# Gate rows through TensorE and PSUM instead of a scatter, and sums and dot products placed behind low parts on VectorE

## The chip, the cores and the metric

The kernel runs on one core of a Trainium2 chip. A core has five engines that run their own instruction lists side by side: PE (TensorE, matmuls; PEld is its weight load), DVE (VectorE), ACT (ScalarE), POOL (GpSimd) and SP (SyncE, which here does nothing but issue transfers). 16 DMA engines move data between the memory of the chip (HBM) and the core's own memories: SBUF (128 partitions) and PSUM (where matmuls accumulate). The metric is the device time of one execution in microseconds (us), lower is better.

## The reference, cut to what matters

One layer of a diffusion transformer: 512 tokens x and 256 context tokens ctx, width 1024, all in float32. A conditioning vector is turned into shifts, scales and gates (nine sections of 1024 numbers for x, from `c`; the same for ctx, from `c_ctx`); they multiply and shift the tokens before a sublayer and scale what the sublayer adds.

```
mod_x = (silu(c) @ w_ada + b_ada).reshape(bsz, N_MOD, 1, d)      # N_MOD = 9
mod_c = (silu(c_ctx) @ w_ada + b_ada).reshape(N_MOD, 1, d)

def ffn_sublayer(h, m, i, w_up, w_down):
    shift, scale, gate = sub_mod(m, i)
    y = swiglu(modulate(h, shift, scale), w_up, w_down)
    return post_ln(DEEPNORM_ALPHA * h + 0.5 * gate * y, ln_g[i], ln_b[i])

x   = ffn_sublayer(x,   mod_x, 0, ffn1_w_in, ffn1_w_out)         # d_ff 2816
ctx = ffn_sublayer(ctx, mod_c, 0, ffn1_w_in, ffn1_w_out)
...                                                              # projections, attention, gated DeltaNet, merge
x   = ffn_sublayer(x,   mod_x, 2, ffn2_w_in, ffn2_w_out)
```

The change touches only how the gates are brought into rows, and when the dot products for `w_ada` and some sums for the first sublayer run. Nothing of what is computed changes.

## The kernel before, in words

**Products in three parts.** Every float32 weight tile that is loaded (128x1024, 512 KB) is split in two: ACT casts a high part (`wh`, the line with `S.copy` in `split`, L137 in the profile) and DVE subtracts it to get a low part (`wl`, L139). Activations are split likewise (`uh`/`ul`, `hx`/`hl`). A product is then three matmuls: high by high, high by low, low by high (L192, L193, L194 in the up-projections, L211 in the down-projections, L521 to L523 in `Seven`). So PE cannot use a weight tile until DVE has made its low part.

**Stages** (by the trace of before): start and modulation of x to 57 us; up-projection of x for the first 8 blocks of the hidden width, the last five of them in 57 to 118 us (called x-up below); the same 8 for ctx, 256 columns wide, 118 to 166 us (ctx-up); the down-projection of x for these 8 to about 226 us (x-down) and of ctx to about 250 us; then 14 blocks for x by a seven-product scheme, class `Seven`, to 460 us; their down-projection for x to 540 us and for ctx until about 600 us with the first layer norms (post_ln, L255 on); projections and convolution to 840 us; gated DeltaNet and attention to 1140 us; merge, second FFN and its down-projection to the end.

**Modulation by dot products.** A section of the conditioning needs 8 tiles of `w_ada` (already transposed, `w_adaT`). The first two sections are done at the start. The other seven come from the generator `ada_gen`: one step (`ada_step`) loads one 512 KB tile by the SP queue (L295) and takes its dot product on DVE (`dot_cols`, L279, a 128x1024 multiply with a running sum) for x and, for sections 2 to 4, a second one for ctx. Steps are called where the other work is expected to leave DVE time: ADA2 and ADA3 list how many per block of `Seven` and per block of the down-projection after it. The result is a column tile: element n of a section lies at partition n % 128, column n // 128.

**Gate rows.** Gates are needed as rows (1024 numbers, the same on all partitions). `to_row` (L239 to L243) halves the 128x8 column tile on ACT into a tile `row`, writes it to HBM with one transfer on SP's queue (`gate<-row`, L243), transposed by its addresses: 128x8 elements of four bytes each. Four rows go this way: section 2 for x and for ctx, section 5 and section 8 for x. `load_g` (L560) and `bcast_row` (L246) later load a row back to all partitions.

**Sums of token blocks.** `Seven` needs sums and differences of blocks of the modulated x tokens: `sums(k)` (L461 and the splits behind it) makes them in four calls, each of four subtractions and four splits: 32 DVE instructions of 128x384 or so in all.

**What sets the order.** The kernel is written with pools of named buffers, and a scheduler that simulates the program by its own estimates of each operation sets the order of the instructions on each engine; buffers of one name are reused in turn, so a load can wait for a reader. `tc.issue_after(x)` puts an instruction behind instruction x in that order. All weight loads, `w_adaT` loads and gate rows share SP's one queue of issues.

Of the kernel before, what the change touches and what calls it, by code (L numbers as in the profile page):

```python
# [10 lines left out]
F32 = mybir.dt.float32  # L11
F32R = mybir.dt.float32r
AF = mybir.ActivationFunctionType
ALU = mybir.AluOpType
# [4 lines left out]
P = 128  # L19
D = 1024  # L20
KT = D // P
# [37 lines left out]
def body(ctx, tc, I, out, dbg=None):  # L59
    nc = tc.nc  # L60
    V, S, G, T = nc.vector, nc.scalar, nc.gpsimd, nc.tensor
# [15 lines left out]
    def tl(p, shape, tag, bufs=1, dt=F32):  # L77
        uid[0] += 1
        return p.tile(list(shape), dt, name=f"{tag}_{uid[0]}", tag=tag, bufs=bufs)
# [54 lines left out]
    def split(src, hi, lo, behind=()):  # L134

        with tc.issue_after(behind[0]) if behind and behind[0] else nullcontext():
            S.copy(hi, src)  # L137
        with tc.issue_after(behind[1]) if behind else nullcontext():
            V.tensor_tensor(lo, src, hi.bitcast(F32), ALU.subtract)  # L139

# [97 lines left out]

    def to_row(sp, cols, row):  # L239

        t = tl(sp, [P, KT], "row")
        S.activation(t[:], cols, AF.Copy, scale=0.5)
        nc.sync.dma_start(row.rearrange("k p -> p k"), t[:])  # L243

# [44 lines left out]
    def ada_gen(tps, raw_of, crow):  # L289
        for sec in range(2, 9):  # L290
            which = [(0, colx)] + ([(1, colc)] if sec < 5 else [])
            sl = slice(sec * 8, sec * 8 + 8)
            for k in range(KT):
                raw = raw_of[0]()
                nc.sync.dma_start(raw[:], I["w_adaT"][sec * KT + k])  # L295
                for w, col in which:
                    dot_cols(tps[0], raw, crow[:, w], col, sec * 8 + k)
                if k < KT - 1:
                    yield
            for w, col in which:  # L300
                V.scalar_tensor_tensor(col[:, sl], col[:, sl], float(sec % 3 == 1), bcol[:, sl], op0=ALU.add, op1=ALU.add)
                if (w, sec) in gates:
                    to_row(tps[0], col[:, sl], gates[(w, sec)])
            yield
# [77 lines left out]
    F0, KC, KL1, KL2 = 3, 2, 6, 6  # L382
    ADA2 = (2,) * 13 + (0,)
    ADA3 = (3, 3, 3, 2, 2, 2, 2, 2)
    PSB = [2]
# [55 lines left out]
    gates = {k: tl(dp, [8, P], "gate")[:] for k in ((0, 2), (1, 2), (0, 5), (0, 8))}  # L441
    ada_tp, ada_raw = [tp], [raw1]
    ada = ada_gen(ada_tp, ada_raw, crow)

    def ada_step(n=1):
        for _ in range(n):
            next(ada, None)

    for f in range(F0, N1):
        hx.append(h_x())  # L450
        ffn_unit(tp, pp, ws.get(), ws.get(), uxh, uxl, NX, *hx[-1])
        for k in range(KC * (f - F0), min(KC * (f - F0 + 1), KT)):
            modulate_k(pp, "c", k)
    ada_step()
    trow = {}
# [13 lines left out]
    for f in range(N1):  # L469
        hc.append(h_c())  # L470
        ffn_unit(tp, pp, ws.get(), ws.get(), uch, ucl, NCT, *hc[-1])
        ada_step(1 - f % 2)
    accd = tl(dp, [6, P, D], "accd")

    def t_sums(j):
        if j < 4:
            sums(j)
        ada_step()
        if j == 3:
            load_g(0)  # L480

    class Seven:
# [43 lines left out]
        def run(self, r):  # L526
# [20 lines left out]
            V.tensor_tensor(c21, c21, self.product(4), ALU.add)  # L547
            V.tensor_tensor(c1[:], c1[:], c2[:], ALU.mult)
            nc.gpsimd.dma_start(hd[self.f - N1].rearrange("p (a n) -> p a n", a=2), c1[:])
# [50 lines left out]
    for f in range(N2):  # L600
        fs[f].run(fs[f + 1] if f + 1 < N2 else None)
        if f + 2 < N2:
            fs.append(Seven(N1 + f + 2))
        ada_step(ADA2[f])
    close_sg()
# [81 lines left out]
    for t in range(4):  # L687
        evac1(lp, bx[t], accx[t], accx[t], gx)
    gc = tl(lp, [P, D], "g")
    bcast_row(gc, gates[(1, 2)])  # L690
# [1170 lines left out]
```

## Time and profile before

| what | before |
|---|---|
| three runs | 1543.77, 1543.99, 1548.96 us; median 1543.99 us |
| profiled execution | 1547.91 us, span of the instructions 1546.1 us, mean granted TensorE clock 0.980 |
| PE busy | 1447.1 us (94% of the span) |
| DVE busy | 1156.1 us (75%) |
| ACT / POOL busy | 648.7 us (42%) / 211.0 us (14%) |
| DMA | 248.03 MB, 160 GB/s over the span |

PE is busy nearly all of the time and can be slowed only by what it waits for and by its clock. The stages differ, though: in some, DVE is nearly as busy as PE. A row of a timeline reads: start, duration, engine, line, operation, out<-in, shapes, count, and in brackets how long the engine stood idle before and what released it. Matmul rows with a count cover several in a row. A row of the windows reads: stretch, its length, then for each engine the busy time and (in brackets) the instructions, the granted TensorE clock, the busy share of the DMA engines and their GB/s.

### The profile page before, as it was taken

Reading aid. Unit: us, or ns where it says so; the run is one execution under the profiler, and the core shown is the slowest. Engines: PE = TensorE matmul, PEld = TensorE weight load, DVE = VectorE, ACT = ScalarE, POOL = GpSimd, SP = SyncE. Lnnn points to the kernel's source line nnn. Section 1 sums busy time; section 2 is a strip of 40 time slices with the busy share of each in tenths; the row PEclk is TensorE's granted clock in tenths of the full one; section 3 lists DMA queues with packets and bytes.
Section 4 is the critical chain, followed back from the end, with each engine's and each line's share of the span. In section 5 each row is a group of like instructions: output and inputs, shape, how many; then the busy total and the mean of one; then the engine's idle time right before and its main releaser. Section 6 shows DMA issues by size and latency. Waiting matters only on the chain.

```text
span 1546.1 us, 23871 instructions
## 1 busy us (share of the span) xinstructions
PE 1447.1 (94%) x9114; PEld 1266.2 (82%) x9114; DVE 1156.1 (75%) x1992; ACT 648.7 (42%) x1067; POOL 211.0 (14%) x251
## 2 busy tenths in 40 slices
PE   6998979999989978999997899989999999999997
PEld 4778859999987866888875687867778999998886
DVE  8787748999976777587767886566668799886426
ACT  5444313334333144555643444266625454344310
POOL 0000000000010012132300101143232022220001
PEclk9999989999999999999999999999999999999999
DMA  9666785445549763232277443173353233324422
GB/s 370 207 242 203 180 256 179 170 154 196 173 146 381 239 167 121 88 109 79 92 220 214 152 127 121 62 259 114 110 189 122 84 110 123 110 99 147 137 82 82
DMA packets 118852, 248.03 MB, mean 160 GB/s; under 512 B 39201, under 2 KB 54609, under 8 KB 118737
## 3 DMA queue, kind: packets, MB, share of 16 engines
q1 hardware_dynamic: 113728, 227.30, 45.4%
q0 software_dynamic: 3424, 13.90, 2.3%
q10 hardware_dynamic: 1586, 5.32, 0.9%
q8 instruction: 71, 1.16, 0.3%
q14 instruction: 43, 0.35, 0.1%
HBM read 214.98 MB, written 31.50 MB: 159 GB/s over the span
## 4 chain that ended last, share of the span: by engine, by line
PE 48%; DVE 17%; DMA 16%; issue 14%; ACT 3%; POOL 2%; SPq 1%; DVEq 0%; POOLq 0%; ACTq 0%
PE ps L211 9%; PE pm L192 4%; PE pm L194 4%; PE pm L193 4%; DMA wr<-in_dn_dram 4%; DVE wl L139 3%; PE ps L1649 3%; PE ps L1648 3%; PE ps L1650 3%; PE pc L1018 2%; PE ps L192 2%; PE ps L194 2%; PE ps L193 2%; DVE adap L279 2%; DMA wr<-in_w_adaT_dram 2%
## 5 line engine op out<-in xcount | busy, mean ns | idle before, releaser
L139 DVE TENSOR_TENSOR wl<-wr,wh 128x1024 fp32r<-128x1024 f32 (+1 forms) x187 | 228.0, 1223 | 116.7 <-ACT wh L137 116.5
L137 ACT CAST wh<-wr 128x1024 fp32r<-128x1024 f32 (+1 forms) x187 | 188.7, 1013 | 270.0 <-PE pm L193 61.1
L192 PE MATMUL pm<-uxh,wh 128*128 128x512 f32 x320 | 133.1, 416 | 2.6 <-ACT u L151 1.9
L194 PE MATMUL pm<-uxh,wl 128*128 128x512 f32 x320 | 127.8, 399 | 0.7 <-DVE wl L139 0.7
L193 PE MATMUL pm<-uxl,wh 128*128 128x512 f32 x320 | 127.3, 398 | 0.0
L279 DVE SCALAR_TENSOR_TENSOR adap<-wr,crow 128x1024 f32<-128x1024 f32 x86 | 104.7, 1218 | 18.2 <-DMA wr<-in_w_adaT_dram 17.5
L211 PE MATMUL ps<-wh,hx 128*128 128x512 f32 x352 | 97.4, 396 | 2.2 <-ACT wh L137 2.2
L114 POOL TENSOR_TENSOR rs<-ve,mhalf 128x1 f32<-128x1 f32 (+2 forms) x46 | 50.5, 1102 | 336.0 <-DVE ve L110 328.8
L211 PEld LDWEIGHTS ps<-wh,hx 128*128 128x128 f32 x352 | 67.0, 191 | 17.4 <-ACT wh L137 3.1
L192 PEld LDWEIGHTS pm<-uxh,wh 128*128 128x128 f32 x320 | 61.5, 192 | 14.8 <-ACT u L151 2.1
L194 PEld LDWEIGHTS pm<-uxh,wl 128*128 128x128 f32 x320 | 61.2, 191 | 15.0 <-DVE wl L139 1.9
L194 PE MATMUL ps<-uh,wl 128*128 128x256 f32 (+1 forms) x208 | 67.8, 326 | 4.2 <-DVE wl L139 4.2
L193 PEld LDWEIGHTS pm<-uxl,wh 128*128 128x128 f32 x320 | 61.6, 193 | 10.4
L193 PE MATMUL ps<-ul,wh 128*128 128x256 f32 (+1 forms) x208 | 67.1, 323 | 1.2 <-DVE ul L139 1.2
L192 PE MATMUL ps<-uh,wh 128*128 128x256 f32 (+1 forms) x208 | 67.7, 325 | 0.0
L192 PE MATMUL ps<-uxh,wh 128*128 128x256 f32 (+1 forms) x192 | 60.6, 324 | 6.4 <-ACT uxh L137 6.4
L211 PE MATMUL ps<-wl,hx 128*128 128x512 f32 x176 | 56.1, 398 | 9.3 <-DVE wl L139 9.3
L521 PE MATMUL ps<-uh,wh 128*128 128x384 f32 x168 | 57.5, 342 | 6.0 <-ACT c L530 5.0
L193 PE MATMUL ps<-uxl,wh 128*128 128x256 f32 (+1 forms) x192 | 60.7, 319 | 0.9 <-DVE uxl L139 0.9
L194 PE MATMUL ps<-uxh,wl 128*128 128x256 f32 (+1 forms) x192 | 60.5, 318 | 0.0
L522 PE MATMUL ps<-ul,wh 128*128 128x384 f32 x168 | 57.1, 340 | 0.0
L523 PE MATMUL ps<-uh,wl 128*128 128x384 f32 x168 | 57.1, 341 | 0.0
(479 smaller groups left out, 4191.1 us busy)
## 6 DMA issues: line engine op xcount, KB each, us to landing
wr<-in_w_adaT_dram SPq DMA_DIRECT2D x69, 512.0 KB, 4.5
wr<-in_up_dram SPq DMA_DIRECT2D x57, 512.0 KB, 3.3
wr<-in_dn_dram SPq DMA_DIRECT2D x53, 512.0 KB, 3.8
wr<-in_win_dram SPq DMA_DIRECT2D x52, 512.0 KB, 3.5
ra<-in_up_dram SPq DMA_DIRECT2D x23, 512.0 KB, 4.0
ra<-in_w_adaT_dram SPq DMA_DIRECT2D x19, 512.0 KB, 4.6
rb<-in_up_dram SPq DMA_DIRECT2D x18, 512.0 KB, 3.6
wr<-in_w_o_dram SPq DMA_DIRECT2D x8, 512.0 KB, 4.3
```

The lines of the kernel that those rows point to most:

```text
L114: G.tensor_tensor(rs[:], ve[:], mhalf[:, 0:n], ALU.pow)
L137: S.copy(hi, src)
L139: V.tensor_tensor(lo, src, hi.bitcast(F32), ALU.subtract)
L192: T.matmul(ps, a, uh[:, k, :], start=(k == 0), stop=False)
L193: T.matmul(ps, a, ul[:, k, :], start=False, stop=False)
L194: marks["mm"] = T.matmul(ps, b, uh[:, k, :], start=False, stop=(k == nk - 1)).ins
L211: T.matmul(banks[t][d][:, c0:c1], a[:, sl], b[:, d * 512 + c0:d * 512 + c1], start=first and j == 0, stop=last and j == 2)
L279: V.scalar_tensor_tensor(pr[:], raw[:], 1.0, crow, op0=ALU.mult, op1=ALU.mult, accum_out=col[:, c:c + 1])
L521: T.matmul(ps[:], a, mh, start=k == 0, stop=False)
L522: T.matmul(ps[:], a, ml, start=False, stop=False)
L523: T.matmul(ps[:], b, mh, start=False, stop=k == 3)
L1648: T.matmul(ps[:], a, uh[:, k], start=k == 0, stop=False)
```

## The change

- `to_row` no longer writes a transposed pattern. PE transposes the 128x8 columns into an 8x128 piece of PSUM (L242 of the new kernel), ACT halves that into an SBUF tile, and SP writes eight rows of 512 bytes (L244).
- `ada_gen` no longer calls `to_row`; it puts the finished section on a list, `rows_due`. `rows_out` empties the list at two places: after the up-projection of ctx (section 2 for x and ctx) and after the last down-projected block of x in the first FFN was taken from PSUM (sections 5 and 8 for x).
- Every low part and the last multiply of a `Seven` block now leave a mark. The dot products of a step are put behind the latest low part in DVE's order, and within `Seven` behind that block's last multiply. `sums` is put behind the latest low part at the place where it is called (between the blocks of x-down).
- The steps are dealt out anew: two after x-up (one before), one in each of the first six blocks of ctx-up (every other block before); ADA2 and ADA3 change. By the end of x-down 14 steps are done (11 before), by the end of `Seven` 37 in both, by the end of the down-projection after it all 56 in both.
- The gate row of section 2 is loaded for x after the first block of x-down instead of the fourth.

```diff
         with tc.issue_after(behind[1]) if behind else nullcontext():
-            V.tensor_tensor(lo, src, hi.bitcast(F32), ALU.subtract)
+            marks["lo"] = V.tensor_tensor(lo, src, hi.bitcast(F32), ALU.subtract).ins
...
-    def to_row(sp, cols, row):
-
-        t = tl(sp, [P, KT], "row")
-        S.activation(t[:], cols, AF.Copy, scale=0.5)
-        nc.sync.dma_start(row.rearrange("k p -> p k"), t[:])
+    def to_row(t, pp, cols, row):
+
+        ps = tl(pp, [8, P], "ps", 8)
+        T.transpose(ps[:], cols, ident)
+        S.activation(t, ps[:], AF.Copy, scale=0.5)
+        nc.sync.dma_start(row, t)
...
-                for w, col in which:
-                    dot_cols(tps[0], raw, crow[:, w], col, sec * 8 + k)
+                with tc.issue_after(marks["dot"]):
+                    for w, col in which:
+                        dot_cols(tps[0], raw, crow[:, w], col, sec * 8 + k)
...
-                    to_row(tps[0], col[:, sl], gates[(w, sec)])
+                    rows_due.append((col[:, sl], gates[(w, sec)]))
...
-    ADA2 = (2,) * 13 + (0,)
-    ADA3 = (3, 3, 3, 2, 2, 2, 2, 2)
+    ADA2 = (2,) * 10 + (1, 1, 1, 0)
+    ADA3 = (3, 3, 3, 3, 3, 3, 2, 2)
...
-    def ada_step(n=1):
+    def rows_out(p, tag, bufs):
+        while rows_due:
+            to_row(tl(p, [P, 512], tag, bufs)[0:8, 0:P], pp, *rows_due.pop(0))
+
+    def ada_step(n=1, behind="lo"):
+        marks["dot"] = marks[behind]
         for _ in range(n):
             next(ada, None)
...
-    ada_step()
+    ada_step(2)
...
-        ada_step(1 - f % 2)
+        ada_step(f < 6)
+    rows_out(tp, "fs", 2)
...
     def t_sums(j):
         if j < 4:
-            sums(j)
+            with tc.issue_after(marks["lo"]):
+                sums(j)
         ada_step()
-        if j == 3:
+        if j == 0:
             load_g(0)
...
-            V.tensor_tensor(c1[:], c1[:], c2[:], ALU.mult)
+            marks["h"] = V.tensor_tensor(c1[:], c1[:], c2[:], ALU.mult).ins
...
-        ada_step(ADA2[f])
+        ada_step(ADA2[f], "h")
...
         evac1(lp, bx[t], accx[t], accx[t], gx)
+    rows_out(lp, "h1", 2)
```

How the instructions move, at three places. Numbers behind a name tell its buffer and differ between the two kernels.

**SP around the start of x-down.** The queue of transfers before; `gate` is a row in HBM, `row` the halved column tile, `in_dn_dram` and `in_w_adaT_dram` weights, `fs<-gate` the load of a gate row to all partitions:

```order
L295 DMA wr_1872<-in_w_adaT_dram 128x1024
L243 DMA gate_560<-row_1780 128x8x1
L174 DMA wr_1878<-in_dn_dram 128x1024
L572 DMA hx_1976<-in_x_dram 128x1024
L560 DMA fs_1838<-gate_560 128x512
L243 DMA gate_561<-row_1784 128x8x1
L560 DMA fs_1839<-gate_560 128x512
```

and with the change:

```order
L174 DMA ra_1762<-in_dn_dram 128x1024
L244 DMA gate_560<-fs_1636 8x128
L174 DMA wr_1813<-in_dn_dram 128x1024
L244 DMA gate_561<-fs_1641 8x128
L296 DMA wr_1807<-in_w_adaT_dram 128x1024
L569 DMA fs_1707<-gate_560 128x512
L569 DMA fs_1708<-gate_560 128x512
L581 DMA hx_1990<-in_x_dram 128x1024
```

Both rows are written ahead of the loads that read them, as 8x128, and no row stands between the two loads of the first gate any more.

**SP at the end of the down-projection of x in the first FFN**, where the layer norm's weights `lng` and `lnb` are loaded. Before:

```order
L295 DMA wr_4554<-in_w_adaT_dram 128x1024
L243 DMA gate_563<-row_4559 128x8x1
L251 DMA lng_4752<-in_ln_g_dram 128x1024
L252 DMA lnb_4753<-in_ln_b_dram 128x1024
L246 DMA g_4780<-gate_561 128x1024
```

and with the change:

```order
L296 DMA wr_4521<-in_w_adaT_dram 128x1024
L252 DMA lng_4750<-in_ln_g_dram 128x1024
L253 DMA lnb_4751<-in_ln_b_dram 128x1024
L247 DMA g_4788<-gate_561 128x1024
L244 DMA gate_562<-h_870_4778 8x128
L244 DMA gate_563<-h_872_4783 8x128
```

The gate rows of sections 5 and 8 now stand behind the three loads; before, the row of section 8 stood ahead of them, and that of section 5 within `Seven`.

**DVE at the turn from x-up to ctx-up** (`fs` and `hx` of the last x block, `hc` a hidden block of ctx, `wl` the low parts of the weights of ctx blocks, `ur` the sums of token blocks, `adap` the scratch of a dot product). Before:

```order
L461 TENSOR_TENSOR ur_96<-ur_96 128x384
L272 TENSOR_TENSOR fs_1033<-fs_1033,ps_984 128x512
L461 TENSOR_TENSOR ur_98<-ur_98 128x384
L139 TENSOR_TENSOR ur_1767<-ur_96,ur_1767 128x384
L139 TENSOR_TENSOR wl_1058<-ra_1055,wh_1057 128x1024
L139 TENSOR_TENSOR hx_970<-fs_1033,hx_970 128x512
L139 TENSOR_TENSOR wl_1126<-wr_1123,wh_1125 128x1024
L272 TENSOR_TENSOR fs_1111<-fs_1111,ps_1062 128x256
L279 SCALAR_TENSOR_TENSOR adap_1260,colx_72<-ra_1258,crow_83 128x1024
L139 TENSOR_TENSOR wl_1132<-wr_1129,wh_1131 128x1024
```

and with the change:

```order
L273 TENSOR_TENSOR fs_1033<-fs_1033,ps_984 128x512
L139 TENSOR_TENSOR wl_1064<-ra_1061,wh_1063 128x1024
L139 TENSOR_TENSOR hx_970<-fs_1033,hx_970 128x512
L280 SCALAR_TENSOR_TENSOR adap_1040,colx_72<-wr_1038,crow_83 128x1024
L280 SCALAR_TENSOR_TENSOR adap_1042,colc_73<-wr_1038,crow_83 128x1024
L280 SCALAR_TENSOR_TENSOR adap_1046,colx_72<-wr_1044,crow_83 128x1024
L273 TENSOR_TENSOR fs_1117<-fs_1117,ps_1068 128x256
L280 SCALAR_TENSOR_TENSOR adap_1048,colc_73<-wr_1044,crow_83 128x1024
L139 TENSOR_TENSOR hc_1054<-fs_1117,hc_1054 128x256
L280 SCALAR_TENSOR_TENSOR adap_1124,colx_72<-wr_1122,crow_83 128x1024
L139 TENSOR_TENSOR wl_1132<-wr_1129,wh_1131 128x1024
```

The sums are gone from x-up, and the second low part of ctx's second block (the last row, `wl_1132`; the same tile ends the list before) now stands behind five dot products.

More of the change, by code (lines that the diff above doesn't have):

```diff
@@ L441, in body @@
     gates = {k: tl(dp, [8, P], "gate")[:] for k in ((0, 2), (1, 2), (0, 5), (0, 8))}
-    ada_tp, ada_raw = [tp], [raw1]
+    ada_tp, ada_raw, rows_due = [tp], [raw1], []
     ada = ada_gen(ada_tp, ada_raw, crow)
-    def ada_step(n=1):
+    def rows_out(p, tag, bufs):
[3 more added lines that the diff above has]
+        marks["dot"] = marks[behind]
         for _ in range(n):
```

## The prediction

> **What bounds the kernel now.** I read the page's busy shares first, the slices and the chain of waits next.
>
> ```profile
> PE 1447.1 (94%) x9114; PEld 1266.2 (82%) x9114; DVE 1156.1 (75%) x1992; ACT 648.7 (42%) x1067; POOL 211.0 (14%) x251
> PE   6998979999989978999997899989999999999997
> PE 48%; DVE 17%; DMA 16%; issue 14%; ACT 3%; POOL 2%; SPq 1%; DVEq 0%; POOLq 0%; ACTq 0%
> ```
>
> PE is busy 94% of the span, so an edit here can win only PE's idle time and its clock. PE's slices (38.7 us each) dip near 200 us, at 425 and at 550, and DVE and DMA hold a third of the chain. The timeline of PE shows what the dips are.
>
> ```profile
> 212.63 1.22 PE L211 MATMUL ps<-wl,hx 128*128 128x512 f32 x2 [8.74 <-DVE wl L139]
> ...
> 218.60 1.09 PE L211 MATMUL ps<-wh,hx 128*128 128x512 f32 x4
> 219.53 0.62 PE L211 MATMUL ps<-wl,hx 128*128 128x512 f32 x2
> ...
> 431.51 0.69 PE L521 MATMUL ps<-uh,wh 128*128 128x384 f32 x1 [4.98 <-ACT c L530]
> ...
> 436.79 0.36 PE L522 MATMUL ps<-ur,wh 128*128 128x384 f32 x1
> ...
> 553.30 1.22 PE L211 MATMUL ps<-wl,hc 128*128 128x512 f32 x2 [7.20 <-DVE wl L139]
> ...
> 557.08 0.62 PE L211 MATMUL ps<-wl,hc 128*128 128x512 f32 x2
> ```
>
> Three stalls of 8.74, 4.98 and 7.20 us, 20.92 together, each with slow matmuls behind it: four take 0.93 us from 218.60 on, but the 14 from 212.63 to 218.60 took 5.97. Next the timelines of the engines that ended the stalls, and of SP's queue.
>
> ```profile
> 196.03 0.38 SPq L243 DMA_DIRECT2D gate<-row  x1
> ...
> 208.94 1.22 DVE L279 SCALAR_TENSOR_TENSOR adap<-ra,crow 128x1024 f32<-128x1024 f32 x1 [10.84 <-DMA ra<-in_w_adaT_dram]
> ...
> 211.35 1.22 DVE L139 TENSOR_TENSOR wl<-wr,wh 128x1024 fp32r<-128x1024 f32 x1
> 212.49 1.22 DVE L139 TENSOR_TENSOR wl<-ra,wh 128x1024 fp32r<-128x1024 f32 x1
> ...
> 413.92 0.38 SPq L243 DMA_DIRECT2D gate<-row  x1
> ...
> 430.98 0.48 ACT L530 COPY c<-ps 128x384 f32<-128x384 f32 x1 [9.01 <-DMA hd<-c]
> ...
> 539.43 0.38 SPq L243 DMA_DIRECT2D gate<-row  x1
> 539.90 1.33 SPq L251 DMA_DIRECT2D lng<-in_ln_g_dram  x1
> ...
> 550.83 1.28 DVE L257 SCALAR_TENSOR_TENSOR ax<-ax,bmv,lng 128x1024 f32<-128x1024 f32 x1 [7.17 <-DMA lng<-in_ln_g_dram]
> ```
>
> Each stall ends with a transfer under way beside or behind a gate row, and none of the three (a `w_ada` tile, `hd<-c`, `lng`) needs the row. Last, the row's own transfers, and windows ahead of, during and after them.
>
> ```profile
> L243 SPq DMA_DIRECT2D gate<-row x4: 378/378/385, 183.0 to 539.4; - x4
> DMA to landing us min/median/max: 9.2/10.8/12.6
> ...
> 171.00:183.00 12.00, 12.00 (x54) 9.73 (x53) 11.89 (x22) 3.55 (x8) 0.00 (x0) 1.00 0.55 180
> 196.40:208.00 11.60, 6.62 (x27) 4.73 (x26) 1.23 (x1) 1.49 (x2) 0.00 (x0) 1.00 0.94 115
> 422.00:426.00 4.00, 4.00 (x24) 4.00 (x24) 1.29 (x2) 0.00 (x0) 0.00 (x0) 1.00 0.37 70
> 426.00:430.00 4.00, 0.53 (x4) 0.21 (x2) 1.70 (x3) 0.00 (x0) 0.00 (x0) 1.00 1.01 393
> 539.80:550.30 10.50, 6.30 (x28) 4.88 (x26) 3.82 (x8) 2.10 (x2) 0.56 (x1) 0.96 0.92 50
> ```
>
> 4 KB are 9.2 to 12.6 us in flight, and meanwhile all transfers together move 50 to 115 GB/s (180 just before the first row); when the third row is through, 393. The four-byte writes hold up what is behind them: that is the bound at these three places.
>
> **The change part by part.** The sum is made against the profiled execution, 1547.91 us (span 1546.1), which is 3.9 above the median of the runs, 1543.99.
>
> *Gate rows.* Eight rows of 512 bytes replace 1024 elements of four. The trace has no such transfer; its price lies between a hold-up of nothing and the old 9.2 us. It is nearer to the ordinary loads, so I take nothing, and the three stalls go: 20.92. So does the clock behind them. At 0.93/4 = 0.23 us each, 14 matmuls take 3.2 instead of 5.97 (2.8 lost). From 431.51 to 436.79 stand 16 of 384 columns; at 0.23 x 384/512 = 0.17 they take 2.75 instead of 5.28 (2.5 lost). Behind the third stall ten took 3.78 against 2.3 (1.5 lost). Together 6.8, so **-27.7**. The four new transposes, shorter than a 512-column matmul of 0.23, cost under 1 us, and ACT's passes are four as before: 0.
>
> [...]
>
> *Sums.* They leave x-up, where DVE is nearly full, for x-down.
>
> ```profile
> 57.60:127.70 70.10, 66.03 (x312) 53.22 (x311) 60.94 (x115) 30.45 (x54) 0.00 (x0) 1.00 0.66 225
> 118.30:165.00 46.70, 42.38 (x348) 41.46 (x349) 38.03 (x59) 21.73 (x32) 0.00 (x0) 1.00 0.63 211
> ...
> L461 DVE TENSOR_TENSOR ur<-ur,ur 128x384 f32<-128x384 f32 x8 | 4.2, 550 | 0.0
> L139 DVE TENSOR_TENSOR ur<-ur,ur 128x384 fp32r<-128x384 f32 x8 | 4.2, 550 | 0.0
> L461 DVE TENSOR_TENSOR ur<-ur 128x384 f32<-128x384 f32 x8 | 4.2, 549 | 0.0
> L139 DVE TENSOR_TENSOR hx<-fs,hx 128x512 fp32r<-128x512 f32 x8 | 5.5, 685 | 0.8 <-ACT hx L137 0.7
> ...
> 112.50 0.50 PE L194 MATMUL ps<-uh,wl 128*128 128x512 f32 x1 [0.87 <-DVE wl L139]
> ...
> 146.37 0.39 PE L194 MATMUL ps<-uh,wl 128*128 128x256 f32 x1 [1.37 <-DVE wl L139]
> ...
> 198.16 0.73 PE L211 MATMUL ps<-wl,hx 128*128 128x512 f32 x2 [0.53 <-DVE wl L139]
> ```
>
> 24 of the 32 instructions (the three groups of `ur`) run in 57 to 128 us: 12.6 of DVE's 60.9. Without them DVE is well ahead, and the six stalls of PE on a low part between 112 and 147 us (first and last shown), 5.4 together, should go: **-5.4** (0 to -5.4).
>
> In x-down these 24 come to the eight already there. A block is 24 matmuls of 0.23, 5.5 us of PE. DVE steps on every 1.14 us through 128x1024 tiles (211.35, 212.49: 0.08 less than they last), so 0.47 through 128x384. A block with sums and a step of two dots costs it 1.14 + 8 x 0.47 + 2.3 = 7.2, four such are 6.8 behind PE; the next two, at 3.4, win back 4.2. The tail's low parts are then up to 2.6 late; about 1 of it I give to low parts made ahead: 1.7 against the 0.9 of small stalls there now (the largest shown). **+0.8** (0 to +5 with nothing won back).
>
> *Dot products bound.* At the turn to ctx-up the second block's second low part, `wl_1132`, stands behind five dots. From the gated product of the last x block on: 0.68, 1.22, 0.68, three dots and two at 1.2, two of 128x256 at under 0.55, itself 1.22, together 10.9. PE reaches that low part after three products of 24 matmuls at 0.12 (42.38/348) and two more: 8.8. **+2.3** (0 to +5, if the dots' tiles come late). After that a ctx block costs DVE two low parts, two dots and two instructions of 256 columns at some 0.4, 5.4 us, against 48 x 0.12 = 5.8 of PE: it keeps up. In `Seven` three steps of two dots become steps of one, and what was three of one is earlier: 3 x 2.3 = 7 us less, which I count as 0, since PE waits there for the row alone.
>
> *End of the down-projection of x.*
>
> ```profile
> 543.50 0.15 DVE L110 TENSOR_SCALAR ve<-bmv 128x1 f32<-128x1 f32 x1
> wr<-in_dn_dram SPq DMA_DIRECT2D x53, 512.0 KB, 3.8
> ```
>
> `lng`, issued at 539.90 without a row ahead, lands 3.8 (the median of such loads) to 5 us later, up to 1.5 after the statistics at 543.65 want it, and the first low part now stands behind the second normalising pass, 1.28, too. Of the stall removed, **+2.5** come back (0 to 4).
>
> Sum: -27.7 - 5.4 + 0.8 + 2.3 + 2.5 = **-27.5**. On the profiled execution 1520.4, on the median 1516.5; I say 1517. Its own range is 1510 (new stalls at nothing, and about 1 more) to 1527 (two of them at their upper bound, or x-up's stalls staying and one of them).
>
> **The rivals.**
>
> ```profile
> DVE adap L279 <- DMA ra<-in_w_adaT_dram: 22.8, 8, 10.8
> DVE adap L279 <- DMA wr<-in_w_adaT_dram: 17.5, 10, 4.0
> ```
>
> *1. The wait moves into DVE's order.* Dots waited for their tile 18 times, 40.3 us, 2.24 each. Placed behind one low part, a dot stands ahead of the next, and a late tile holds that. If five steps of ctx-up and x-down pass their 2.24 to PE, it is 11 more: 1528. For it: DVE is at 94% of PE in ctx-up by the count above. Against it: the longest wait, 10.84, was itself behind a gate row. [...]
>
> *2. Slower.* The same place at its worst: all 14 steps before `Seven` pass 2.24 on (31 us), and three of the stalls grow to where the clock halves (6.8 as above): 38 more than the forecast, 1555. It decides from 27 us of new waits on. Against it: where no row is in flight the DMA engines were 0.55 to 0.66 busy, and PE lost 5.4 us to late low parts in all of 112 to 147.
>
> *3. Later stages reshuffled.* The scheduler's own times change a little for all that follows.
>
> ```profile
> 640.00:1546.00 906.00, 860.94 (x6133) 748.64 (x6131) 648.36 (x1153) 396.16 (x695) 177.94 (x191) 0.99 0.39 127
> ```
>
> PE idles 45 us in these 906; a quarter more is 11: 1528. A gain there is as likely, and in the range.
>
> *4. The change doesn't do what it says:* the loads were slow by their own crowding, and half of the 27.7 stays: 1531. For it: before 426 the DMA engines were not full (0.37). Against it: 70 GB/s with loads waiting, and 393 once the row was through.
>
> **How the numbers follow.** Forecast 0.60, rival 1 0.18, rival 3 0.09, rival 4 0.07, rival 2 0.06. The range 1506 to 1533 takes in the forecast's own and rivals 1, 3 and 4; its low end is a gain of 4 in the later stages on top. What can be told from no change is 0.5%, 7.7 us: faster is below 1536.3, all cases but rival 2 and some tails, 0.90; same 0.05, slower 0.05.
>
> **What would show it.** Right: 8x128 rows that land in 2 to 5 us; no stall of PE over 3 us and no half clock near 200 to 220, 425 to 437 and 545 to 558; no waits for `wl` from 112 to 118, and one of about 2 us soon after 118. Wrong: low parts that follow a dot waiting for its tile in many blocks of 118 to 226 (rivals 1 and 2); rows that take 9 us, or `lng` landing after 550 again (4); more than 45 us of PE idle after 640 (3).

## The result

The changed kernel took **1524.60 us** (median of 4, 1524.11 to 1525.88) against **1545.01 us** (median of 4, 1543.77 to 1548.96) for the kernel before beside it: ratio 0.9865, 95% interval 0.9845 to 0.9885, 20.4 us less. The prediction was 1517, range 1506 to 1533, its own range 1510 to 1527. The profiled execution's span went from 1546.1 to 1522.6 us, 23.5 less, where the sum of the prediction had 27.5.

The page of the changed kernel, busy shares, slices of PE and DVE, and the chain of waits:

```profile
PE 1442.9 (95%) x9118; PEld 1265.1 (83%) x9118; DVE 1161.1 (76%) x1992; ACT 648.8 (43%) x1067; POOL 209.6 (14%) x251
PE   6999999999999988999996999989999999999997
DVE  8768888999977895768777796567669799886426
PE 65%; DVE 13%; DMA 12%; issue 4%; ACT 3%; POOL 2%; SPq 1%; DVEq 0%; ACTq 0%; POOLq 0%
```

The dips of PE near 200 and 425 us are gone, the one near 550 is shallower (8 tenths instead of 7); PE holds 65% of the chain instead of 48%. PE's timeline shows every stall over 0.5 us between 60 and 577 us:

```profile
95.31 0.50 PE L194 MATMUL ps<-uh,wl 128*128 128x512 f32 x1 [0.62 <-DVE wl L139]
...
108.63 0.50 PE L194 MATMUL ps<-uh,wl 128*128 128x512 f32 x1 [1.61 <-DVE wl L139]
...
129.04 0.39 PE L192 MATMUL ps<-uh,wh 128*128 128x256 f32 x1 [1.11 <-ACT wh L137]
...
130.30 0.58 PE L194 MATMUL ps<-uh,wl 128*128 128x256 f32 x1 [0.75 <-DVE wl L139]
...
205.04 3.57 PE L211 MATMUL ps<-wh,hx 128*128 128x512 f32 x8 [2.08 <-ACT wh L137]
...
462.42 2.11 PE L211 MATMUL ps<-wh,hx 128*128 128x512 f32 x8 [2.05 <-ACT wh L137]
...
530.77 0.73 PE L211 MATMUL ps<-wl,hc 128*128 128x512 f32 x2 [1.17 <-DVE wl L139]
...
552.64 0.73 PE L211 MATMUL ps<-wl,hc 128*128 128x512 f32 x2 [0.75 <-DVE wl L139]
...
577.04 1.65 PE L192 MATMUL ps<-uxh,wh 128*128 128x512 f32 x3 [9.64 <-ACT uxh L137]
```

The stalls of 8.74, 4.98 and 7.20 us have no successor of their size (the last row is the layer norm's tail, 6.43 us in the kernel before). New are 95.31, 108.63, 129.04, 130.30 and 205.04; gone with the three are the six small stalls on low parts between 112 and 147 us, 5.4 together. A table by stages, from the first matmul of each stage in the two profiled executions, shows where the time went:

| stage | before | changed | difference | prediction |
|---|---|---|---|---|
| start, x-up, ctx-up | 169.0 | 170.0 | +1.0 | -3.1 |
| x-down | 56.9 | 47.7 | -9.2 | -10.7 |
| ctx-down | 21.8 | 21.8 | 0.0 | 0 |
| Seven | 213.5 | 204.4 | -9.1 | -7.5 |
| down-projection of x | 78.4 | 79.1 | +0.7 | 0 |
| that of ctx, layer norms | 61.1 | 54.1 | -7.0 | -6.2 |
| projections, convolution | 250.1 | 248.3 | -1.8 | 0 |
| DeltaNet and attention (to the merge's first matmul with a low part) | 261.3 | 264.3 | +3.0 | 0 |
| the rest | 434.0 | 433.0 | -1.0 | 0 |

(x-down's forecast is the first stall and its clock, 11.5, less 0.8; that of Seven the second stall and its clock; that of the layer norms the third, 8.7, less 2.5.)

Gate rows in the new kernel, in SP's timeline, and what the transfers beside them took (160 to 200 us: copies, size, median us from issue to landing):

```profile
171.26 0.35 SPq L244 DMA_DIRECT2D gate<-fs  x1
...
172.88 0.29 SPq L244 DMA_DIRECT2D gate<-fs  x1
...
174.76 2.37 SPq L569 DMA_DIRECT2D fs<-gate  x2
...
528.11 0.89 SPq L244 DMA_DIRECT2D gate<-h  x2
...
wr<-in_dn_dram SPq DMA_DIRECT2D x4, 512.0 KB, 4.2
ra<-in_w_adaT_dram SPq DMA_DIRECT2D x2, 512.0 KB, 4.3
```

The load of the first row leaves at 174.76, 3.5 us after the row's write was issued; before it was 12.6 (183.00 to 195.60). The load of the second row leaves at 176.81, released by the landing of the row that was written at 172.88: that is 3.9 us, within the 2 to 5 that the prediction named as a sign. Weights beside it land after 4.2 us.

### The profile page after: what moved, and what is told of

Same layout as the page of the kernel before. It is cut to its first block, busy times and chain, and to the rows that moved or that the text cites. A ratio compares the mean times of both kernels' runs of the same rounds, so it can differ in the third digit from the quotient of the medians.

```text
span 1522.6 us, 23874 instructions
## 1 busy us (share of the span) xinstructions
PE 1442.9 (95%) x9118; PEld 1265.1 (83%) x9118; DVE 1161.1 (76%) x1992; ACT 648.8 (43%) x1067; POOL 209.6 (14%) x251
## 4 chain that ended last, share of the span: by engine, by line
PE 65%; DVE 13%; DMA 12%; issue 4%; ACT 3%; POOL 2%; SPq 1%; DVEq 0%; ACTq 0%; POOLq 0%
PE ps L211 12%; PE ps L531 4%; PE ps L530 4%; PE ps L532 4%; PE pm L192 4%; PE pm L193 4%; PE pm L194 4%; PE ps L1659 3%; PE ps L1658 3%; PE ps L1660 3%; DVE wl L139 3%; DMA wr<-in_w_adaT_dram 3%; PE ps L194 3%; PE ps L193 3%; PE ps L192 3%
## 5 line engine op out<-in xcount | busy, mean ns | idle before, releaser
L139 DVE TENSOR_TENSOR wl<-wr,wh 128x1024 fp32r<-128x1024 f32 (+1 forms) x183 | 224.0, 1228 | 115.2 <-ACT wh L137 114.8
L137 ACT CAST wh<-wr 128x1024 fp32r<-128x1024 f32 (+1 forms) x183 | 184.4, 1012 | 292.8 <-PE pm L193 60.3
L280 DVE SCALAR_TENSOR_TENSOR adap<-wr,crow 128x1024 f32<-128x1024 f32 x92 | 112.1, 1219 | 13.9 <-DMA wr<-in_w_adaT_dram 13.2
L192 PEld LDWEIGHTS pm<-uxh,wh 128*128 128x128 f32 x320 | 61.2, 191 | 12.9 <-ACT spill L777 1.9
L137 ACT CAST wh<-ra 128x1024 fp32r<-128x1024 f32 x32 | 33.7, 1052 | 75.1 <-issue 16.9
L193 PE MATMUL ps<-uxl,wh 128*128 128x256 f32 (+1 forms) x192 | 61.1, 320 | 1.0 <-DVE uxl L139 0.9
L530 PE MATMUL ps<-ur,wh 128*128 128x384 f32 x168 | 56.5, 336 | 0.0
L531 PE MATMUL ps<-ur,wh 128*128 128x384 f32 x168 | 56.4, 336 | 0.0
```

Of the source, the lines that this page charges most:

```text
L139: marks["lo"] = V.tensor_tensor(lo, src, hi.bitcast(F32), ALU.subtract).ins
L192: T.matmul(ps, a, uh[:, k, :], start=(k == 0), stop=False)
L193: T.matmul(ps, a, ul[:, k, :], start=False, stop=False)
L280: V.scalar_tensor_tensor(pr[:], raw[:], 1.0, crow, op0=ALU.mult, op1=ALU.mult, accum_out=col[:, c:c + 1])
L530: T.matmul(ps[:], a, mh, start=k == 0, stop=False)
L531: T.matmul(ps[:], a, ml, start=False, stop=False)
```

## Experiments

The runs were made in three sets, each with the kernel before beside it on the same chip. It took 1553.99, 1553.35 and 1544.61 us there (medians), so totals of different sets are compared by their ratio to it. Stage times are from one profiled execution of each kernel; between executions of the same code they differ by up to 1.5 us where this can be compared (with nothing bound, x-down starts at 169.4, 170.9 and 170.9). "Bound" means placed behind another instruction by `tc.issue_after`, "free" that the scheduler alone places it.

**Gate rows and dealing alone, nothing bound.**

```diff
-            with tc.issue_after(marks["lo"]):
-                sums(j)
+            sums(j)
...
-                with tc.issue_after(marks["dot"]):
-                    for w, col in which:
-                        dot_cols(tps[0], raw, crow[:, w], col, sec * 8 + k)
+                for w, col in which:
+                    dot_cols(tps[0], raw, crow[:, w], col, sec * 8 + k)
```

> The changed kernel without its two bindings: the sums and the dot products go wherever the scheduler puts them, while the gate rows over TensorE and the new dealing of the steps stay. Theory A (the gate rows carry the whole gain; what is missing of the forecast was lost where sums and dots are bound): 1515 to 1521, so faster than the changed kernel by 4 or more. Rival B (the bindings matter little, and the missing part lies in stalls that were hidden under the old ones): 1522 to 1529, within 4 of the changed kernel, with a stall of about 2 us before the last two blocks of x-down still there. Rival C (the bindings carry a large part of the gain): over 1532.

1520.38 us, beside 1553.99 for the kernel before: ratio 0.9777 (0.9748 to 0.9806), better than the changed kernel's 0.9865. x-down takes 43.6 us instead of 47.7, with no stall at its end. Theory A's direction is right, but over two sets a few us can't be settled, so the two were run side by side:

> The changed kernel once more, on the chip of the runs beside it, as their measure: 1520 to 1530, the stall of 2 us before the last two blocks of x-down with half clock behind it again.

> The kernel with the new gate rows and the new dealing but with neither sums nor dots bound, beside the changed kernel on one chip. Theory A (binding both costs: x-down 4 us shorter without, the rest from other orders later): 2 to 6 us faster than the changed kernel beside it. Rival (the gap seen between the two came from different chips): within 2 us of it.

On one chip: the changed kernel 1528.01 us (ratio 0.9827, 0.9810 to 0.9845), with nothing bound 1519.64 (0.9779, 0.9761 to 0.9798). In the repeat of the changed kernel the stall of 2.08 us is there again, but no half clock behind it. The kernel without the two bindings is 8.4 us faster, more than theory A's 2 to 6, and the intervals lie apart. The gap is real, and the bindings as a whole cost. Where, the stages say: x-down 46.8 against 43.7; Seven 204.4 against 205.9, in favour of binding; projections and convolution 250.8 against 247.6; and DeltaNet with attention, from their first 32x32 product to the same matmul of the merge, in two windows (the changed kernel first, then the kernel with nothing bound):

```profile
828.04:1102.95 274.91, 256.25 (x2354) 207.40 (x2354) 190.87 (x411) 134.56 (x294) 59.76 (x87) 0.96 0.42 133
```

```profile
822.58:1090.69 268.11, 255.02 (x2354) 206.92 (x2355) 187.18 (x411) 134.49 (x294) 60.29 (x87) 0.96 0.43 136
```

The same 2354 matmuls, 6.8 us apart, of which 5.6 are idle time of PE (18.7 against 13.1). This stage begins some 300 us behind the last bound instruction; the end of this section comes back to it. So of the 12.3 us between the two profiled spans (1528.0 and 1515.7), only 1.6 lie in x-down and Seven, where the bindings stand, and 10.0 in the projections and in this stage, which no binding touches.

**Sums free, dot products bound.**

```diff
-            with tc.issue_after(marks["lo"]):
-                sums(j)
+            sums(j)
```

> The changed kernel with the sums alone not bound behind low parts. Theory A (moving the sums out of x-up did not shorten it, because DVE waits there for tiles of w_ada and the sums fill those waits): x-up and ctx-up within 1.5 us of the changed kernel's (first matmul of x-down at 170.0), the whole within 4 of 1524.6. Rival B (the sums were in the way in x-up, as the prediction had it): first matmul of x-down 3 or more us later, the whole 3 to 6 slower. Rival C (bound sums make the dots late in x-down and so the stall before its last two blocks): that stall of 2.08 us goes, the whole 2 to 5 faster.

1530.27 us, ratio 0.9851 (0.9816 to 0.9886). The first matmul of x-down comes at 171.9, 1.9 later than in the changed kernel (the code up to there gave 169.1 to 170.3 in four executions), between theory A (within 1.5) and rival B (3 or more): the sums did stand in the way in x-up, by about 1.9 and not by the predicted 5.4. The stall at x-down's end is gone, x-down takes 43.7. Ctx-down starts 2.1 earlier than in the changed kernel (215.6 against 217.7). So rival C's mechanism holds in x-down; its gain is not seen in the total: the down-projection of x takes 1.7 us more than in the changed kernel, DeltaNet and attention 0.8, what follows them 1.9.

**Dot products free, sums bound.**

```diff
-                with tc.issue_after(marks["dot"]):
-                    for w, col in which:
-                        dot_cols(tps[0], raw, crow[:, w], col, sec * 8 + k)
+                for w, col in which:
+                    dot_cols(tps[0], raw, crow[:, w], col, sec * 8 + k)
```

> The changed kernel with the dot products alone not bound behind low parts. Theory A (bound dots hold the raw tiles' buffers longer, so that weights that share these buffers are loaded later): the stalls of PE in 95 to 131 and 157 to 159 us, together 5 us, shrink by 2 or more and the half clock after 129 goes, the whole 3 to 6 faster. Rival B (the scheduler's own places are as good or worse): within 3 of 1524.6, or slower with new stalls in Seven, where the changed kernel has none.

1524.05 us, ratio 0.9804 (0.9771 to 0.9837). Theory A fails at the turn to ctx-up, whose stalls did not shrink but grew:

```profile
124.95 0.39 PE L194 MATMUL ps<-uh,wl 128*128 128x256 f32 x1 [2.78 <-DVE wl L139]
...
132.44 0.58 PE L194 MATMUL ps<-uh,wl 128*128 128x256 f32 x1 [4.49 <-DVE wl L139]
```

With sums bound and dots free the scheduler puts dots ahead of low parts there; these dots wait 3.26 and 4.51 us for their tiles (at 121.27 and 130.01 on DVE), and x-down starts at 175.8, 5.8 later. x-down itself takes 43.8 us. Seven has a stall of 1.08 us again, as rival B had it. So up to the end of ctx-up binding the dots is worth some 5 us as long as the sums are bound, and nothing when they are free (171.9 against 169.4 to 170.9 with nothing bound); and the two bindings together cost 3 to 4 in x-down. Either one alone does not.

**What makes the stall at the end of x-down.**

```diff
         if j < 4:
             with tc.issue_after(marks["lo"]):
                 sums(j)
-        ada_step()
+            ada_step()
...
-    ADA2 = (2,) * 10 + (1, 1, 1, 0)
+    ADA2 = (2,) * 12 + (1, 0)
```

> The changed kernel with no step of dot products in the last two of x-down's blocks that call one; one step more in each of two late Seven blocks instead. Theory A (two late steps hold the raw tiles' buffers that the last two down-projection weights need): the stall of 2.08 us before these two blocks and the half clock behind it go, x-down takes 43.7 us instead of 47.7, the whole 2 to 5 faster than the changed kernel beside it, and Seven stays without stalls. Rival B (the sums, not the steps, make those low parts late): x-down stays above 46. Rival C (the stall was hidden under the one removed and belongs to the buffers of the high parts alone): stays too.

1523.23 us beside the changed kernel's 1528.01, ratio to the kernel before 0.9795 (0.9777 to 0.9813). The stall is gone, x-down takes 43.6: theory A, but for Seven, which has a stall of 1.38 us at 378.2 and takes 206.1 us instead of 204.4. (The total, 4.8 us less, can't be put down to the stall alone: beside the repeat of the changed kernel, x-down takes 3.2 less, the start 1.9 more, Seven 1.7 more, the down-projection of x 1.0 more, and DeltaNet and attention, in another order, 6.1 less.) What happens there in the changed kernel, by the timelines of SP, ACT and DVE (one execution; DVE's row and SP's rows first, then ACT's):

```profile
197.86 1.21 DVE L280 SCALAR_TENSOR_TENSOR adap<-wr,crow 128x1024 f32<-128x1024 f32 x1
...
199.10 0.33 SPq L174 DMA_DIRECT2D wr<-in_dn_dram  x1
...
202.99 0.33 SPq L581 DMA_DIRECT2D hx<-in_ctx_dram  x1
203.41 0.38 SPq L174 DMA_DIRECT2D wr<-in_dn_dram  x1
...
203.00 1.04 ACT L137 CAST wh<-ra 128x1024 fp32r<-128x1024 f32 x1 [7.01 <-PE ps L211]
203.95 1.04 ACT L137 CAST wh<-wr 128x1024 fp32r<-128x1024 f32 x1
```

The tile for the last but one block (`wr`, 199.10) leaves in the moment in which a dot product releases a buffer of the same name: raw tiles of weights and of `w_ada` take five buffers in turn, three of them named `wr`. It is cast at 203.95 and PE goes on at 205.04. The trace does not give the landing of this tile; with the 4.3 us of a load of `ra` beside it, it comes at 203.4 (an estimate), so the cast could start 0.5 us earlier at most. (ACT's 7.01 us of idle before 203.00 ended with PE's last matmul, not with a load.) So the late instruction there is not the low part, as the prediction had it, but the load, which waits for a dot. The dot is late because DVE has no pause left, 18.77 us busy of 19:

```profile
184.00:203.00 19.00, 18.96 (x84) 15.38 (x82) 18.77 (x34) 4.56 (x9) 0.00 (x0) 1.00 0.68 238
```

Without the late steps a stall of 4.58 us is new at 535.68, in the down-projection of ctx, where the changed kernel has 1.17; the layer norm's tail in turn is 2.85 and 2.66 instead of 9.64, and the stage as a whole is 1.8 us shorter (52.5 against 54.2).

**The old four-byte write at the new places.**

```diff
-        ps = tl(pp, [8, P], "ps", 8)
-        T.transpose(ps[:], cols, ident)
-        S.activation(t, ps[:], AF.Copy, scale=0.5)
-        nc.sync.dma_start(row, t)
+        S.activation(t, cols, AF.Copy, scale=0.5)
+        nc.sync.dma_start(row.rearrange("k p -> p k"), t)
```

> The changed kernel with the old four-byte writes of the gate rows, at the new places, all else as it is. Theory A (the writes hold up everything behind them): two rows at the start of x-down and two at the end of the down-projection of x bring stalls of PE back: 5 us or more at each of the two places with half clock behind, 1537 to 1555 in all; loads issued behind a row land after 9 us or more. Rival (the loads were slow by their own crowding, and the new places alone would do): within 4 of the changed kernel's 1524.6.

1547.93 us, ratio 0.9956 (0.9938 to 0.9974), as theory A says: the stalls are back at the new places. PE's stalls, and a window while the rows are under way:

```profile
200.26 1.22 PE L211 MATMUL ps<-wh,hx 128*128 128x512 f32 x2 [8.96 <-ACT wh L137]
...
220.16 3.78 PE L211 MATMUL ps<-wh,hx 128*128 128x512 f32 x8 [6.75 <-ACT wh L137]
...
559.30 2.08 PE L211 MATMUL ps<-wh,hc 128*128 128x512 f32 x4 [6.21 <-ACT wh L137]
...
178.00:190.00 12.00, 12.00 (x54) 9.95 (x53) 8.93 (x17) 4.15 (x9) 0.00 (x0) 1.00 0.15 19
```

21.9 us of stalls; for 12 us all loads together move 19 GB/s. The form of the write decides, not its place: this kernel differs from the changed one in the write alone (and in the orders that follow), and its span is 1543.9 against 1522.6.

**The price of a row by pieces and by queue.** Two kernels add three writes each to the changed kernel, in Seven, to rows in HBM that nobody reads, each when a section is finished. The first:

```diff
+                    if sec == 3:
+                        nc.sync.dma_start(d.rearrange("k (a b) -> (k a) b", a=16), cs)
+                    if sec == 4:
+                        nc.sync.dma_start(d.rearrange("k p -> p k"), cs)
+                    if sec == 5:
+                        nc.sync.dma_start(d[0:2].rearrange("k p -> p k"), cs[:, 0:2])
```

> The changed kernel with three more writes on SP's queue, to rows that nobody reads, at three places in Seven: 128 pieces of 32 bytes (one per partition), 1024 pieces of 4 bytes (the old gate row), 256 pieces of 4 bytes. Theory A (what holds up is the number of pieces): they land after 2 to 4, 9 to 13 and 3 to 5 us; only the second holds up loads (landing after 9 or more) and stalls PE, by 3 to 6 us with half clock behind. Rival (the stall comes from crowding by the other loads at its place): the second lands after 9 us or more but Seven's PE goes on without a stall over 1 us. In all 1525 to 1536.

The windows behind the three writes (128 pieces of 32 bytes at 269.0, 1024 of four bytes at 345.9, 256 of four bytes at 402.9):

```profile
269.00:274.00 5.00, 5.00 (x31) 5.00 (x30) 5.00 (x10) 2.41 (x4) 0.00 (x0) 1.00 0.47 119
274.00:279.00 5.00, 5.00 (x31) 5.00 (x30) 3.71 (x5) 1.99 (x3) 0.54 (x1) 1.00 0.53 197
...
350.90:355.90 5.00, 5.00 (x31) 5.00 (x30) 1.79 (x3) 0.00 (x0) 0.00 (x0) 1.00 0.60 23
355.90:360.90 5.00, 5.00 (x31) 5.00 (x30) 1.23 (x2) 0.00 (x0) 0.00 (x0) 1.00 0.55 31
...
407.90:412.90 5.00, 5.00 (x31) 5.00 (x30) 5.00 (x9) 1.33 (x2) 0.54 (x1) 1.00 0.69 28
```

32-byte pieces did nothing that can be seen: 119 and 197 GB/s, against 105 and 210 in the same stretches of the changed kernel, and the `w_ada` tile beside them landed after 3.4 us. The old row took the bandwidth down to 23 and 31 GB/s for ten us, where the changed kernel has 247 and 188; loads beside it took 12.9 and 13.3 us. But so did a quarter of it: with 256 pieces 28 GB/s (158 in the changed kernel), and 10.4 us for the `w_ada` loads around it (median). The number of pieces isn't the measure, against theory A. PE's stalls were small here (1.53 us at 363.61, 0.62 at 419.38): it seems that in the middle of Seven enough is loaded ahead. The whole took 1530.93 us.

The second:

```diff
+                    if sec == 3:
+                        nc.scalar.dma_start(d.rearrange("k p -> p k"), cs)
+                    if sec == 4:
+                        nc.gpsimd.dma_start(d.rearrange("k p -> p k"), cs)
+                    if sec == 5:
+                        nc.sync.dma_start(d[0:4].rearrange("k p -> p k"), cs[:, 0:4])
```

> The changed kernel with three more writes in four-byte pieces in Seven, to rows that nobody reads: 1024 pieces from ACT's queue, 1024 from POOL's, 512 from SP's. Theory A (the pieces hold the transfers behind them on their own queue): loads on SP's queue go on at 3 to 5 us and above 150 GB/s beside the first two, and stand behind the third as they did behind 256 and 1024 pieces. Rival B (the writes hold up the memory or all DMA engines, whatever the queue): the bandwidth falls to 10 to 60 GB/s for about ten us in all three.

The windows behind the writes from ACT's queue (issued at 267.68), POOL's (347.26) and SP's with 512 pieces (401.00), and POOL's write itself:

```profile
272.70:277.70 5.00, 5.00 (x31) 5.00 (x30) 3.88 (x5) 1.90 (x3) 0.55 (x1) 1.00 0.16 26
...
352.30:357.30 5.00, 5.00 (x31) 5.00 (x30) 3.06 (x5) 0.01 (x1) 0.00 (x0) 1.00 0.45 32
...
406.00:411.00 5.00, 5.00 (x31) 5.00 (x30) 5.00 (x9) 1.33 (x2) 0.54 (x1) 1.00 0.60 37
...
dead<-colx POOLq DMA_DIRECT2D x1, 4.0 KB, 10.2
```

26, 32 and 37 GB/s over all queues: rival B. The four-byte pieces slowed the transfers beside them from each of the three queues, and not on their own queue alone: `hd<-c`, on POOL's queue, landed after 7.7 us beside ACT's write and after 7.3 beside SP's, against a median of 2.7 in 230 to 450 us of the changed kernel. 1525.83 us in all. Neither of the other two queues would have been a remedy here.

**Binding in Seven alone, and one step fewer early.** Both start from the kernel with nothing bound, which was run beside them:

> The kernel with the new gate rows and the new dealing, nothing bound, once more as the measure for the two beside it: 1516 to 1524, 2.0 to 2.4% under the kernel before.

1516.78 us beside 1544.61, ratio 0.9812 (0.9786 to 0.9838), 1.9% less and so just short of what was expected.

```diff
-    def ada_step(n=1):
+    def ada_step(n=1, behind=None):
+        marks["dot"] = marks[behind] if behind else None
...
-                for w, col in which:
-                    dot_cols(tps[0], raw, crow[:, w], col, sec * 8 + k)
+                with tc.issue_after(marks["dot"]) if marks["dot"] else nullcontext():
+                    for w, col in which:
+                        dot_cols(tps[0], raw, crow[:, w], col, sec * 8 + k)
```

> The same kernel with the dot products bound behind the block's last multiply within Seven alone; sums, and dots elsewhere, free. Theory A (binding is of use only in Seven, where the kernel with nothing bound has a stall of about 1.1 us that the changed kernel has not, and does harm in ctx-up and x-down): Seven 1.0 to 1.5 us shorter (204.4 instead of 205.9), x-down still 43.7; the whole 0 to 3 faster than the kernel beside it, as far as the later stages keep their length. Rival (which order the scheduler finds for DeltaNet and attention decides more than Seven): the whole moves by 3 or more either way, with a change of that size after 823 us.

1516.82 us, ratio 0.9814 (0.9785 to 0.9844). Seven takes 204.4 us instead of 206.0 and its stall of 1.09 us is gone, as theory A says; the medians can't tell the two kernels apart.

```diff
-    ada_step(2)
+    ada_step()
...
-        ada_step(f < 6)
+        ada_step(f < 7)
```

> The kernel with nothing bound, with one step of dot products after x-up instead of two and one more in ctx-up's seventh block. Theory A (the stalls of PE at the turn to ctx-up, 122 to 130 us, 4.3 us and a half-clock window, come from weights that leave behind the tiles of these steps): they shrink by 2 to 4, first matmul of x-down 2 to 5 us earlier (about 166 to 168.5). Rival (the stalls are set by the number of low parts and loads in that stretch, whoever stands ahead): within 1 us of the kernel beside it.

1519.88 us, ratio 0.9839 (0.9819 to 0.9860): 3.1 us more than the kernel beside it, with intervals that overlap. The first matmul of x-down comes at 171.0 against 170.9: the rival. With nothing bound, whether these steps or the weights stand ahead at the turn to ctx-up matters little: the stalls from 120 us on move (0.72, 1.22, 0.38, 0.98, 0.87 us) and keep their sum, 4.2 against 4.3.

**The stage that nothing touched.** DeltaNet and attention took, from their first 32x32 product to the first matmul of the merge with a low part, 264.3 and 267.5 us in the changed kernel's two profiles, 265.1 with the sums free, 266.1 and 265.4 with the added rows; but 261.3 before, 259.0, 260.7 and 259.5 with nothing bound, 259.3 with the old write, 262.9 with dots free, 261.4 without the late steps, 258.7 with one step less early. PE's instructions of this stage stand in one and the same order in the first five executions, and in one other order, that of the kernel before, in the other eight (but for a few 32x32 products, which with the old write and with dots free stand a few places off). The means are 265.7 and 260.4: 5.3 us go with the scheduler's other order. (The kernel bound in Seven alone has a third order and took 259.9.) The code of the stage is the same in all of them. That the length goes with the order is shown. Of the 5.3, 2.1 are idle time of PE in the stage (16.5 us in the mean against 14.4); the granted clock is lower too in the mean, 0.964 against 0.973, but not in every execution: with nothing bound it was 0.957 once, and the stage took 260.7. Which waits make the difference, and why the scheduler finds this order, was not followed further.

## Why the prediction was right, point by point

The mechanism that carries the forecast, the gate rows, held. That the whole came within 4.1 us of it is in part luck: in the table above the stages miss by +9.3 and by -5.2 us, and these cancel in part.

- **Gate rows, -27.7: right in mechanism and nearly in size.** At the three places 20.92 us of stall and 6.8 of clock went; 2.08 and 1.7 of clock came in their place at x-down's end, and 1.17 at the layer norms. The old write at the new places brought 21.9 us of stalls back. The price of an 8x128 row was taken as no hold-up, and that held: `wr` loads beside it took 4.2 us. Rival 4 (crowding) falls with the same run.
- **The clock behind stalls.** In the kernel before, the granted clock stood at 0.50 behind the three stalls of 4.98 to 8.74 us and at 1.00 behind one of 1.89 (at 479.57). The prediction priced the stalls of about 2 us that it expected without a half clock; that was its estimate. The trace of the changed kernel shows both: at 462.42 the clock stayed at 1.00 behind a stall of 2.05, but behind 205.04 eight matmuls took 3.57 us after a stall of 2.08, 1.5 more than the 2.11 of the second row below, and the half clock lasted 3.4 us, 1.7 lost in all; another such window followed 129.04 (granted clock 0.96 in the first row). In the repeat the stall at x-down's end left the clock alone (second row), as in two more executions with the same code up to there. x-down took 46.8 us in the repeat against 47.7, only 0.9 less, since PE, faster there, waited 0.48 us for the next low part (third row):

```profile
118.30:165.00 46.70, 43.95 (x349) 42.91 (x348) 39.84 (x60) 19.93 (x29) 0.00 (x0) 0.96 0.70 234
```

```profile
204.56 2.11 PE L211 MATMUL ps<-wh,hx 128*128 128x512 f32 x8 [2.08 <-ACT wh L137]
...
207.16 0.73 PE L211 MATMUL ps<-wl,hx 128*128 128x512 f32 x2 [0.48 <-DVE wl L139]
```

- **Sums, -5.4: the step that failed.** x-up and ctx-up became 1.0 longer instead of 3.1 shorter, with the dots' +2.3 in it. DVE's load did fall (60.94 to 51.53 us in 57.6 to 127.7), but PE waits there for low parts that stand behind dot products which wait for their tiles. In the changed kernel:

```profile
57.60:127.70 70.10, 67.86 (x333) 55.67 (x332) 51.53 (x94) 26.19 (x45) 0.00 (x0) 1.00 0.68 225
...
92.29 1.23 DVE L280 SCALAR_TENSOR_TENSOR adap<-wr,crow 128x1024 f32<-128x1024 f32 x1 [3.43 <-DMA wr<-in_w_adaT_dram]
93.44 0.68 DVE L273 TENSOR_TENSOR fs<-fs,ps 128x512 f32<-128x512 f32 x1
94.04 1.22 DVE L139 TENSOR_TENSOR wl<-ra,wh 128x1024 fp32r<-128x1024 f32 x1
...
105.61 1.23 DVE L280 SCALAR_TENSOR_TENSOR adap<-ra,crow 128x1024 f32<-128x1024 f32 x1 [4.10 <-DMA ra<-in_w_adaT_dram]
```

  The low part at 94.04 is the one that PE waits for at 95.31. In the kernel before, the same two dots waited less. The first stood behind this low part (there at 90.22) and not ahead of it; the tile of the second was issued at 98.45 instead of 100.12 and landed 2.8 us earlier:

```profile
92.63 1.22 DVE L279 SCALAR_TENSOR_TENSOR adap<-wr,crow 128x1024 f32<-128x1024 f32 x1 [1.18 <-DMA wr<-in_w_adaT_dram]
...
102.84 1.23 DVE L279 SCALAR_TENSOR_TENSOR adap<-ra,crow 128x1024 f32<-128x1024 f32 x1 [1.74 <-DMA ra<-in_w_adaT_dram]
```

  The six old stalls (5.4) went as predicted, but 0.62 and 1.61 in x-up and twice 0.44 late in ctx-up came, 3.1 together. Leaving the sums free, with the dots bound, cost 1.9 us at this place in one execution: about that is what the term was worth, and with the dots free, binding the sums did harm (175.8 against 169.4 to 170.9). The prediction read DVE's busy share (61 of 70 us) as the bound, without asking what DVE waits for between.
- **x-down, +0.8: the size about right, the cause half right.** 2.08 us of stall (1.7 predicted) and 1.7 of clock came. DVE did fall behind under sums and dots, as counted, but what PE waited for was not a low part behind sums: it was a weight's load that waits for a buffer which a bound dot product holds. Bounds 0 to +5 held.
- **Dots at the turn, +2.3:** 1.11 and 0.75 us at 129.04 and 130.30, and a window of half clock, 3.6 in all. Inside its bounds. (The terms shown for it, 10.9 and 8.8, differ by 2.1 and not 2.3.)
- **Seven:** -9.1 against -7.5. With the new rows and dealing but dots free, Seven takes 205.9, which is -7.6. The other 1.5 come from binding the dots behind the block's last multiply, which removes a stall of about 1 us (below, from the kernel before; with nothing bound it is 1.08 us at 364.87); the prediction had counted this as 0:

```profile
376.18 0.41 PE L521 MATMUL ps<-uh,wh 128*128 128x384 f32 x1 [1.01 <-ACT ur L535]
```

- **Layer norms, +2.5 back:** -7.0 against -6.2; `lng` landed 4.1 us after its issue, and 1.17 and 0.75 us of stall stand where the prediction had 2.5. The rest of the stage nearly cancels: stalls of 0.56, 1.05 and 1.06 us went, and the tail grew from 6.43 to 9.64.
- **Rival 1** came true in part: what the two bindings cost together in x-down is 3 to 4 us, by way of a buffer. **Rival 3** came true in mechanism, though PE's idle time in the last 906 us grew by 1.0 only (46.1 against 45.1): 5.3 us by the other order in DeltaNet and attention, 3.0 in the first pair of profiles, made up there by 1.8 less in the projections (a stall of 1.86 us at 633 is gone) and 1.0 later. **Rival 2** did not come.

With rows and dealing alone, nothing bound, the gain beside the kernel before was 33.6, 33.7 and 27.8 us in the three sets: what the prediction gave to the whole change, its gate rows and its dealing do alone. The changed kernel's own gain was 20.4 and, in the repeat, 25.3. Nothing bound is the fastest version that was run beside the changed kernel: 1519.64 against 1528.01 us.

## What to carry to other kernels

Write a row from columns through a transpose on TensorE, since a write in four-byte pieces slowed the other transfers here to 19 to 37 GB/s for some ten us, from whichever of three queues it came. Before work is moved away from a busy engine, ask what the engine waits for in between: work that fills waits costs less than its busy time (here the sums that left x-up, 12.6 us on DVE, were worth about 1.9). Where a scheduler sets orders, look also at stages that the edit doesn't touch: here they moved by 5 us.

## What the hardware showed unexpectedly

- 256, 512 and 1024 four-byte writes held the others up for nearly the same time, eight to ten us at 20 to 40 GB/s; 128 writes of 32 bytes left them at 119 and 197. The small packets themselves were soon through; the hold-up came behind them. With 256 pieces, 288 packets under 512 bytes (the pieces and others) start in 404 to 406 us, and none in the ten us that follow (first and second row):

```profile
DMA packets 379, 0.37 MB, mean 187 GB/s; under 512 B 288, under 2 KB 288, under 8 KB 379
```

```profile
DMA packets 67, 0.27 MB, mean 27 GB/s; under 512 B 0, under 2 KB 0, under 8 KB 67
```

```profile
406.00:416.00 10.00, 10.00 (x60) 10.00 (x58) 8.73 (x15) 2.38 (x3) 0.54 (x1) 1.00 1.02 27
```

  The third row counts the 16 engines as busy all the while (1.02), so each of the 67 packets took 2.4 us on average. With the old write the busy share was as low as 0.15 (178 to 190 us): there the engines were mostly without packets. What holds the transfers up, no run shows.
- A stall of 2.08 us was followed by 3.4 us at half clock in one execution and not in three others with the same code up to there.
